# A hybrid decoder layer on one core: operands queued behind sums, the mix of units in the rotation stage, block sums and mixer weights moved

## Chip, cores and metric

One core of one Trainium2 chip runs the whole program in one launch. The metric is the device time in microseconds (us): the median of the runs. A difference of 0.3% is 5.9 us here.

## What is computed

One layer over 1024 tokens of width 1024, all in float32, batch 1:

```python
h = rmsnorm(x, pre_mix_g)
z = h @ w_in      # columns: GLA q|k|v|out gate|forget, conv B|C|x, dilated q|k|v (1536 each)
y_gla = gla_branch(...)                       # chunked gated linear attention, width 512
y_sc = sc_b * causal_dwconv(sc_c * sc_x, sc_conv_w)
y_dil = dilated_branch(rope(d_q), rope(d_k), d_v)   # 3 groups, dilations 1, 4, 16
proj = stack([y_gla, y_sc, y_dil]) @ w_branch       # each branch 512 -> 1024
gates = sigmoid(h @ w_gate + b_gate)                # 3 x 1024 columns
x = x + rmsnorm(sum(gates * proj) @ w_mix_out, post_mix_g)
h = rmsnorm(x, pre_ffn_g)
gt = causal_dwconv(h @ w_ff_gate, ff_conv_w) + ff_conv_b
y = (gelu(gt) * (h @ w_ff_up)) @ w_ff_down          # 1024 -> 2816 -> 1024
x = x + rmsnorm(y, post_ffn_g)
```

The rotation is `x1*cos - x2*sin`, `x2*cos + x1*sin` on the halves of each head of 128 channels.

## The kernel before

**Numbers in two parts.** Every float32 operand of a matmul is held as a high part (`wh`, `H0h`) and a remainder (`wl`, `H0l`) in a reduced format, and a product is three matmuls: high by high, high by remainder, remainder by high. `split` (L158, L159) makes the parts: ScalarE copies the high part, VectorE subtracts it.

**Units of seven products.** Most projections go through `seven` (L275 on): 256 output channels by 1024 tokens are cut in blocks 2x2x2 and done with seven block products of a Strassen kind in place of eight, each of 12 matmuls of 128x512. Sums of the activations' blocks (`TS`) are made once per stage by `block_sums`. Sums of the weights' blocks are made for each unit on GpSimd: s1 (L291), s2 (L293), s1 again (L295, it overwrites s1, so it waits until VectorE has split the old one) and A21 (L297). On TensorE a unit runs: product into X, the last product of the unit before ("rest"), then Y, Z, X, Z, X. Results are collected in SBUF: ScalarE copies X, Z, X (L314, L319, L322), VectorE adds Y (L316), Z (L325) and X (L327). The rest of a unit writes into bank X once more, so TensorE waits there for L327.

**What is done with a result.** `use` takes each of the four 128x512 quarters. Of a light unit (a gate, GLA's q and k) it is an activation and a store. Of a rotation unit (dilated q and k, `rope_out`, L507 to L528) it is: ScalarE swaps the two halves (L517, L518), VectorE multiplies with the cosine (L524), GpSimd multiplies the swapped copy with the sine (L525), VectorE adds the two (L526), and the quarter is stored.

**Stages**, by time in the profiled execution: norm, transposes and the first gates (0 to 88 us), short convolution and gates (88 to 240), tables of cosine and sine (240 to 268), rotations with light units (268 to 670), v of the dilated branch (670 to 795), GLA (795 to 985), dilated attention (985 to 1175), branches merged and mixed, norms (1160 to 1320), first chunk of the feed-forward and its block sums (1310 to 1360), feed-forward units (to 1750), down projection (to the end).

**Order.** Each engine works its instructions in the order in which a scheduler put them when the kernel was built; `issue_after` tells that scheduler to place an instruction behind another one, and is no wait on the chip. GpSimd, VectorE and ScalarE never pass a waiting instruction. In the rotation stage a loop takes a unit from `turned` (12) or `light` (7) by a rule of shares.

**Mixers.** w_mix_out is loaded in quarters of 512x512 by `mix_unit` in the merge stage, and split there: four parts of 128x1024 on GpSimd (L159 with tiles `mw`, two more for `early`), the last on VectorE. `merge` multiplies gates by branch products on VectorE (L1201) and adds them (L1203), on GpSimd for the first four row tiles.

Of the kernel before, what the change touches and what calls it, by code (L numbers as in the profile page):

```python
# [72 lines left out]
def trunk(ctx: ExitStack, tc, x, positions, w_in, w_alpha_up, b_alpha, gla_norm_g, sc_conv_w,  # L73
# [28 lines left out]
    d_fa = dram.tile([FF // 256, 7, 128, 512], F32, name="d_fa")  # L102
    d_st = [dram.tile([48, 128], F32, name=f"d_st{i}") for i in range(4)]
    d_c = [dram.tile([3, T], F32, name=f"d_c{i}") for i in range(4)]

# [139 lines left out]

    def block_sums(B, scratch, Ts):

        f = lambda h, c, j, cs: B[h][c][:, 4 * j:4 * j + 4, cs].bitcast(F32)
        for q in range(2):
            cs = slice(q * 256, q * 256 + 256)  # L250
            f12, t1, f22, t4 = [scratch[:, i].rearrange("p (k t) -> p k t", k=4) for i in range(4)]
            out = lambda i: (Ts[i][:, 0, :, cs], Ts[i][:, 1, :, cs])
            G.tensor_tensor(f12, f(1, 0, 0, cs), f(1, 1, 0, cs), op=OP.add)
            G.tensor_tensor(f22, f(1, 0, 1, cs), f(1, 1, 1, cs), op=OP.add)
            V.tensor_tensor(t1, f12, f(0, 0, 0, cs), op=OP.subtract)
            V.tensor_tensor(t1, t1, f(0, 1, 0, cs), op=OP.subtract)
            split(*out(0), t1)
            G.tensor_tensor(f12, f22, f12, op=OP.subtract)
            V.tensor_tensor(f22, f22, t1, op=OP.subtract)
            split(*out(1), f22)  # L260
            V.tensor_tensor(t4, f(0, 0, 1, cs), f22, op=OP.subtract)
            G.tensor_tensor(t4, t4, f(0, 1, 1, cs), op=OP.add)
            split(*out(2), f12)
            split(*out(3), t4)

    def seven(src, c0, B, Ts, tmp, dst, use):
# [13 lines left out]
        def made(i, src):  # L280
            with ExitStack() as es:
                if sops:

                    for k in ((2, 1) if i < 2 else (3, 4) if i < 4 else (3, 5)):
                        if k in sums_taken:
                            es.enter_context(tc.issue_after(sums_taken[k].ins))
                split(*op(i), src)
# [219 lines left out]
    S.activation(cos, ac, AF.Sin)  # L507
    seven(w_gate2, 8 * 128, H, TS, STMP, ring, gate_out(8))

# [31 lines left out]
    turned = [(w_in2, col + ch, rope_out(w, ch)) for ch in range(0, 1536, 256) for w, col in enumerate((COL_DQ, COL_DK))]  # L541
    light = [(w_gate2, dt * 128, gate_out(dt)) for dt in range(10, 24, 2)]
    nt, n = len(turned), len(turned) + len(light)
    for i in range(n):
        take = turned if (i + 1) * nt // n > i * nt // n else light
        src, c0, use = take.pop(0)
        seven(src, c0, H, TS, STMP, ring, use)
    seven(w_in2, COL_GQ, H, TS, STMP, ring, gla_out(0))
    seven(w_in2, COL_GK, H, TS, STMP, ring, gla_out(1))


    vops = Ring([wp.tile([128, 2, 4, 256], F32R, name=n, tag=n) for n in ("wh", "wl", "wh", "wl")])
    vsrc = [fr[:, i].rearrange("p (k c) -> p k c", k=4) for i in range(4)]
    vsrc = Ring(vsrc + [rawp.tile([128, 4, 256], F32, name="vsrc", tag="raw") for i in range(3)])
    vout = Ring([slot(t, [128, T], name="vout") for t in ("t0", "t1", "t2")])

    def seven_tok(g):
# [51 lines left out]
        store(c11, 0, 0)  # L609
        Z = [pt("g", "vZ") for h in range(2)]  # L610
        prod(Z, op(add(s1, A[1, 0], A[1, 1], OP.add)), tt(0), True)
        c22 = vout()
        copy(c22, Z)
        prod(X, op(add(s1, s1, A[0, 0])), tt(1), False)
        c12 = vout()
        copy(c12, X)
        prod(Z, op(add(A[0, 1], A[0, 1], s1)), blk(1, 1), False)
        plus(c12, Z)
        store(c12, 0, 1)
        prod(X, op(add(A[1, 0], A[0, 0], A[1, 0])), tt(2), False)  # L620
# [584 lines left out]

    v = w_mix2.rearrange("(k p) c -> p k c", p=128)
# [19 lines left out]
    with tc.issue_after(last["d"]):  # L1226
        mix_unit(0, 1, (mw[:, 0], mw[:, 1]), G)
        for d in range(4):
            merge(d, None, (1,))
            ahead(20 + d)  # L1230
        mix_unit(0, 0, early, G)
    for d in range(4, 8):
        ps = gemm((units[8 + d // 2].h, units[8 + d // 2].l), d % 2 * 128, [(k, k) for k in range(4)], X2, "p2")
        queued(merge, d, ps, on=("s", "v"))
        if d == 5:
            mw = slot("G1", [128, 2, 4, 512], F32R, name="mw")
            mix_unit(1, 1, (mw[:, 0], mw[:, 1]), G)
    queued(mix_unit, 1, 0, late, V, on=("s", "v"))

# [167 lines left out]
    def step_operands(i, c):  # L1407
# [144 lines left out]
```

## Time and profile before

| | |
|---|---|
| median of 3 runs | 1967.72 us (1965.96 to 1971.04) |
| profiled execution, own time | 1971.89 us |
| its span | 1970.1 us |
| mean granted TensorE clock | 0.984 |
| TensorE busy | 1891.7 us, 96% of the span |
| VectorE, ScalarE, GpSimd busy | 67%, 44%, 39% |
| moved by DMA | 251.5 MB |

TensorE leaves 78 us of the span idle. The own time is 1.8 us above the span, and 4.2 us above the median of the three timed runs.

### The profile page before, as it was taken

The page shows a single profiled execution, that of the slowest core. Times are in us where ns is not written, and L with a number is a line of the kernel's source. Part 1 is how long each engine was busy: PE and PEld are TensorE (multiplying, and loading weights), DVE is VectorE, ACT ScalarE, POOL GpSimd, SP SyncE. Part 2 cuts the span into 40 slices and gives each one's busy share as a digit, 9 for nine tenths or more (in the row PEclk, how much of TensorE's full clock was granted, in tenths as well). Part 3 has the DMA queues.
Part 4 walks back from the last instruction along what each step waited for, and adds up shares of the span by engine and source line. Part 5 has one row for each costly group of instructions (what it writes and reads, how often), then busy time and mean ns, then how long its engine had stood idle before and what let it go on. Part 6 is the DMA issues. An engine that isn't in the chain of part 4 may idle for free.

```text
span 1970.1 us, 26193 instructions
## 1 busy us (share of the span) xinstructions
PE 1891.7 (96%) x9649; PEld 1601.9 (81%) x9649; DVE 1317.8 (67%) x1927; ACT 876.2 (44%) x1618; POOL 761.4 (39%) x458
## 2 busy tenths in 40 slices
PE   6999999999999999999999898998999999999998
PEld 5988778888777899899788776886788888878887
DVE  7755675677787433567844568577767777778587
ACT  5433355454444332425456623343443444454453
POOL 4523334545454331102214464016445544516162
PEclk9999999999999999999999998999999999999999
DMA  5121323332322433213477554231223232379763
GB/s 175 65 84 66 123 86 109 106 114 100 111 104 91 139 107 120 75 54 102 121 205 227 160 173 152 95 109 59 99 89 121 94 107 91 118 246 322 263 199 123
DMA packets 187074, 251.54 MB, mean 128 GB/s; under 512 B 30018, under 2 KB 121024, under 8 KB 186945
## 3 DMA queue, kind: packets, MB, share of 16 engines
q1 hardware_dynamic: 186944, 249.86, 38.4%
q8 instruction: 76, 1.25, 0.3%
q14 instruction: 54, 0.43, 0.1%
HBM read 183.34 MB, written 66.47 MB: 127 GB/s over the span
## 4 chain that ended last, share of the span: by engine, by line
PE 70%; DVE 14%; issue 5%; POOL 4%; ACT 4%; DMA 3%; SPq 0%; DVEq 0%; ACTq 0%; POOLq 0%
PE sX L307 21%; PE sZ L307 10%; PE sY L307 6%; PE fX L1496 6%; PE fY L1496 4%; PE vX L586 4%; DVE wl L159 3%; PE vZ L586 2%; PE mx L1253 1%; PE mx L1254 1%; PE mx L1252 1%; PE gs L768 1%; PE p L198 1%; POOL fr L525 1%; PE p L200 1%
## 5 line engine op out<-in xcount | busy, mean ns | idle before, releaser
L159 DVE TENSOR_TENSOR wl<-raw,wh 128x512 fp32r<-128x512 f32 (+1 forms) x214 | 215.7, 1044 | 111.4 <-ACT wh L158 108.5
L307 PE MATMUL sX<-T,wh 128*128 128x512 f32 x720 | 227.1, 397 | 10.9 <-DVE ring L327 10.2
L158 ACT ACTIVATE wh<-raw 128x512 fp32r<-128x512 f32 (+1 forms) x226 | 146.2, 671 | 82.2 <-PE sX L307 42.8
L307 PEld LDWEIGHTS sX<-T,wh 128*128 128x128 f32 x720 | 136.7, 191 | 44.0 <-DVE ring L327 14.4
L307 PE MATMUL sX<-FT,wh 128*128 128x512 f32 x480 | 150.1, 394 | 5.9 <-DVE ring L327 4.1
L307 PE MATMUL sX<-T,wl 128*128 128x512 f32 x360 | 142.1, 395 | 0.0
L525 POOL TENSOR_TENSOR fr<-fr 128x512 f32<-128x512 f32 x48 | 70.6, 1471 | 147.7 <-ACT fr L518 146.3
L307 PEld LDWEIGHTS sX<-FT,wh 128*128 128x128 f32 x480 | 89.7, 189 | 28.6 <-DVE ring L327 8.6
L159 DVE TENSOR_TENSOR wl<-fr,wh 128x512 fp32r<-128x512 f32 x90 | 67.0, 766 | 64.3 <-ACT wh L158 63.5
L158 ACT ACTIVATE wh<-fr 128x512 fp32r<-128x512 f32 (+1 forms) x97 | 61.7, 657 | 77.7 <-PE sX L307 49.0
L307 PE MATMUL sX<-FT,wl 128*128 128x512 f32 x240 | 94.1, 392 | 0.0
L291 POOL TENSOR_TENSOR fr<-raw 128x512 f32<-128x512 f32 x30 | 42.0, 1401 | 123.2 <-DMA raw<-in_w_gate_dram 44.6
L159 DVE TENSOR_TENSOR ops<-rw,ops 128x512 fp32r<-128x512 f32 x72 | 62.9, 902 | 30.4 <-ACT ops L158 30.0
L307 PEld LDWEIGHTS sX<-T,wl 128*128 128x128 f32 x360 | 68.8, 191 | 14.8
L297 POOL TENSOR_TENSOR raw<-raw 128x512 f32<-128x512 f32 x50 | 78.3, 1566 | 0.0
L1319 POOL TENSOR_TENSOR fb<-fb 128x512 f32<-128x512 f32 x40 | 61.7, 1543 | 42.4 <-DVE fb L1368 33.9
L526 DVE TENSOR_TENSOR ring<-ring,fr 128x512 f32<-128x512 f32 x48 | 55.2, 1149 | 29.7 <-POOL fr L525 28.2
L307 PE MATMUL sZ<-T,wh 128*128 128x512 f32 x240 | 73.9, 389 | 0.0
L1496 PE MATMUL fX<-ops 128*128 128x512 f32 x312 | 73.2, 389 | 0.0
L1496 PEld LDWEIGHTS fX<-ops 128*128 128x128 f32 x312 | 58.6, 188 | 12.2
L158 ACT ACTIVATE ops<-rw 128x512 fp32r<-128x512 f32 x72 | 43.2, 626 | 55.5 <-PE fX L1496 23.3
L295 POOL TENSOR_TENSOR fr<-raw,fr 128x512 f32<-128x512 f32 x30 | 49.7, 1656 | 46.5 <-DVE wl L159 46.5
(553 smaller groups left out, 5617.4 us busy)
## 6 DMA issues: line engine op xcount, KB each, us to landing
rw<-in_w_ff_down_dram SPq DMA_DIRECT2D x99, 256.0 KB
raw<-in_w_in_dram SPq DMA_DIRECT2D x48, 512.0 KB
rw<-d_fa SPq DMA_DIRECT2D x77, 256.0 KB
d_fa<-fb SPq DMA_DIRECT2D x70, 256.0 KB
raw<-in_w_gate_dram SPq DMA_DIRECT2D x24, 512.0 KB
d_sig<-ring SPq DMA_DIRECT2D x48, 256.0 KB
d_qk<-ring SPq DMA_DIRECT2D x48, 256.0 KB
raw<-in_w_ff_gate_dram SPq DMA_DIRECT2D x22, 512.0 KB
```

Of the source, the lines that this page charges most:

```text
L158: S.activation(h, src, AF.Copy)
L159: eng.tensor_tensor(l, src, h.bitcast(F32), op=OP.subtract)
L198: PE.matmul(ps[h], a, xs[h][0][:, kx, :], start=st, stop=False)
L291: G.tensor_tensor(s1, A21, A22, op=OP.add)
L295: G.tensor_tensor(s1, A12, s2, op=OP.subtract)
L297: G.tensor_tensor(A21, A11, A21, op=OP.subtract)
L307: PE.matmul(ps, a[x][:, k], b[y][:, k], start=first and k == 0 and n == 0, stop=k == 3 and n == 2, skip_group_check=not first)
L525: G.tensor_tensor(sw, sw, sin[:, hs], op=OP.mult)
L526: V.tensor_tensor(as_(o), as_(o), perm(sw), op=OP.add)
L586: PE.matmul(o, b[y][:, k, ts], a[:, x, k], start=first and t % 2 == 0 and k == 0 and n == 0, stop=k == 3 and n == 2, skip_group_check=not ...
L1319: G.tensor_tensor(o, p, q, op=op)
L1496: PE.matmul(P[t], o[:, a, ts], o[:, b], start=st, stop=c + k == NCH - 1 and x == 2, skip_group_check=i not in (2, 1, 5))
```

## The change

1. `made` in `seven` queues each operand's split behind a sum of the unit before in every stage; before, only where `sops` was filled (the feed-forward). Operands 0 and 1 go behind the unit's L319 and L316, 2 and 3 behind L322 and L325, 4 to 6 behind L322 and L327.
2. A second gate unit runs in the stage of the tables, GLA's q and k join the list `light`, and the rule rounds up.
3. The mixers' weights are loaded, split and stored to `d_mw` in 16 steps of 128x512 inside the v stage; `mix_unit` then only loads the finished parts. The steps take the third raw buffer of the v stage.
4. The feed-forward's `block_sums` makes its two f12 sums on VectorE, not on GpSimd.
5. In the down projection operands of all but the first two steps are queued behind the last unit's L327.

```diff
-    def block_sums(B, scratch, Ts):
+    def block_sums(B, scratch, Ts, E=G):
-            G.tensor_tensor(f12, f(1, 0, 0, cs), f(1, 1, 0, cs), op=OP.add)
             G.tensor_tensor(f22, f(1, 0, 1, cs), f(1, 1, 1, cs), op=OP.add)
+            E.tensor_tensor(f12, f(1, 0, 0, cs), f(1, 1, 0, cs), op=OP.add)
...
-            G.tensor_tensor(f12, f22, f12, op=OP.subtract)
+            E.tensor_tensor(f12, f22, f12, op=OP.subtract)
...
         def made(i, src):
             with ExitStack() as es:
-                if sops:
-
-                    for k in ((2, 1) if i < 2 else (3, 4) if i < 4 else (3, 5)):
-                        if k in sums_taken:
-                            es.enter_context(tc.issue_after(sums_taken[k].ins))
+                for k in ((2, 1) if i < 2 else (3, 4) if i < 4 else (3, 5)):
+                    if k in sums_taken:
+                        es.enter_context(tc.issue_after(sums_taken[k].ins))
                 split(*op(i), src)
...
-    seven(w_gate2, 8 * 128, H, TS, STMP, ring, gate_out(8))
+    for dt in (8, 10):
+        seven(w_gate2, dt * 128, H, TS, STMP, ring, gate_out(dt))
...
-    light = [(w_gate2, dt * 128, gate_out(dt)) for dt in range(10, 24, 2)]
+    light = [(w_gate2, dt * 128, gate_out(dt)) for dt in range(12, 24, 2)]
+    light += [(w_in2, COL_GQ, gla_out(0)), (w_in2, COL_GK, gla_out(1))]
...
-        take = turned if (i + 1) * nt // n > i * nt // n else light
+        take = turned if -(-(i + 1) * nt // n) > -(-i * nt // n) else light
...
-    seven(w_in2, COL_GQ, H, TS, STMP, ring, gla_out(0))
-    seven(w_in2, COL_GK, H, TS, STMP, ring, gla_out(1))
...
-    vsrc = Ring(vsrc + [rawp.tile([128, 4, 256], F32, name="vsrc", tag="raw") for i in range(3)])
+    vsrc = Ring(vsrc + [rawp.tile([128, 4, 256], F32, name="vsrc", tag="raw") for i in range(2)])
+    mws = rawp.tile([128, 2, 512], F32R, name="mws", tag="raw")
+
+    def mix_weights():
+
+        v = w_mix2.rearrange("(n i k p) c -> n i k p c", n=1, i=2, p=128)[0]
+        x = mws[:, 0].bitcast(F32)
+        for n in range(2):
+            for i in range(2):
+                for k in range(4):
+                    nc.sync.dma_start(x, v[i, k][:, n * 512:n * 512 + 512])
+                    split(mws[:, 1], mws[:, 0], x)
+                    for part in range(2):
+                        nc.sync.dma_start(d_mw[n, i, part][:, k], mws[:, 1 - part].bitcast(F32))
+                    yield
...
+        next(mixing, None)
...
-    def mix_unit(n, i, pool, eng):
-        mixw[n][i] = wunit([v[:, 4 * i + 2 * j:4 * i + 2 * j + 2, n * 512:n * 512 + 512] for j in range(2)], [4, 512],
-                           pool=pool, eng=eng)
+    def mix_unit(n, i, pool):
+        u = mixw[n][i] = W()
+        u.h, u.l = pool
+        for part in range(2):
+            nc.sync.dma_start(pool[part].bitcast(F32), d_mw[n, i, part])
...
-    queued(mix_unit, 1, 0, late, V, on=("s", "v"))
+    mix_unit(1, 0, late)
...
-    block_sums(F, fb, FT)
+    block_sums(F, fb, FT, V)
...
-        split(o[:, 0], o[:, 1], a)
-        split(o[:, 2], o[:, 3], b)
+
+        with tc.issue_after(sums_taken[5].ins) if len(ready) > 1 else nullcontext():
+            split(o[:, 0], o[:, 1], a)
+            split(o[:, 2], o[:, 3], b)
```

The next two blocks are VectorE's queue over one rotation unit that stands behind a rotation unit (dilation 4 or 16), before and then after the change; the names are tiles, `ring` a quarter, `fr` scratch and tables, `wl<-raw` and `wl<-fr` remainders of the next unit's operands.

```order
L316 TENSOR_TENSOR ring<-ring,sY 128x512
L526 TENSOR_TENSOR ring<-ring,fr 128x512
L524 TENSOR_TENSOR ring<-fr,ring 128x512
L526 TENSOR_TENSOR ring<-ring,fr 128x512
L159 TENSOR_TENSOR wl<-raw,wh 128x512 x2
L159 TENSOR_TENSOR wl<-fr,wh 128x512 x2
L325 TENSOR_TENSOR ring<-ring,sZ 128x512
L524 TENSOR_TENSOR ring<-fr,ring 128x512
L327 TENSOR_TENSOR ring<-ring,sX 128x512
L526 TENSOR_TENSOR ring<-ring,fr 128x512
```

```order
L318 TENSOR_TENSOR ring<-ring,sY 128x512
L529 TENSOR_TENSOR ring<-ring,fr 128x512
L527 TENSOR_TENSOR ring<-fr,ring 128x512
L529 TENSOR_TENSOR ring<-ring,fr 128x512
L161 TENSOR_TENSOR wl<-raw,wh 128x512 x2
L327 TENSOR_TENSOR ring<-ring,sZ 128x512
L161 TENSOR_TENSOR wl<-fr,wh 128x512
L527 TENSOR_TENSOR ring<-fr,ring 128x512
L161 TENSOR_TENSOR wl<-fr,wh 128x512
L529 TENSOR_TENSOR ring<-ring,fr 128x512
L329 TENSOR_TENSOR ring<-ring,sX 128x512
```

The changed file's lines are two or three higher: L161 is the old L159, L318 is L316, L327 is L325, L329 is L327, L527 is L524 and L529 is L526. What moved: the sum of Z stands ahead of both `wl<-fr` splits, and the sum of X now stands behind the rotation's add L529, where it stood ahead of it. In all 12 rotation units X has one such add ahead of it. GpSimd's queue is the same inside a unit: s1, s2, A21, s1 again (L295), then the products with the sine (L525). In sequence the stage was, behind the gate of the tables, L T L T T L T T L T L T T L T T L T T, then q and k (T a rotation, L a light unit); it is now, behind two gates, four times T T L T L, of which the last two L are q and k. Rotations behind a rotation were five, and are four.

Next is GpSimd's queue in the merge stage, before and then after: `mw` and `wl` with L159 are mixer weights, `dE` and `cH1l` belong to the branches, `m_...` and `dB` are merged row tiles.

```order
L1033 TENSOR_TENSOR dD<-dD,cH1l 128x1024
L1036 TENSOR_TENSOR cH1l<-dD 128x1024
L1102 TENSOR_TENSOR dE<-dE,sg 128x1024 x3
L159 TENSOR_TENSOR mw<-raw,mw 128x1024 x2
L1203 TENSOR_TENSOR dB<-dB,m_7233 128x512 x4
L1203 TENSOR_TENSOR m_9064<-m_9064,m_7234 128x512 x2
L1203 TENSOR_TENSOR m_9065<-m_9065,m_7234 128x512 x2
L159 TENSOR_TENSOR wl<-raw,wh 128x1024 x2
L159 TENSOR_TENSOR mw<-raw,mw 128x1024 x2
```

```order
L1061 TENSOR_TENSOR dD<-dD 128x1024
L1058 TENSOR_TENSOR dD<-dD,cH1l 128x1024
L1061 TENSOR_TENSOR cH1l<-dD 128x1024
L1127 TENSOR_TENSOR dE<-dE,sg 128x1024 x3
L1228 TENSOR_TENSOR dB<-dB,m_7314 128x512 x4
L1228 TENSOR_TENSOR m_9145<-m_9145,m_7315 128x512 x2
L1228 TENSOR_TENSOR m_9146<-m_9146,m_7315 128x512 x2
```

The two splits ahead of the merges' adds (L1203, now L1228) and the four behind them are gone; GpSimd's next work are the block sums of the feed-forward.

Last, VectorE's queue where the down projection begins, before and then after: `ops`, `wh<-rw`, `wl<-rw` are its operands, L1368 (now L1394) multiplies a gate.

```order
L316 TENSOR_TENSOR ring<-ring,sY 128x512
L1368 TENSOR_TENSOR fb<-fb,ring 128x512
L159 TENSOR_TENSOR ops<-rw,ops 128x512 x8
L159 TENSOR_TENSOR wh<-rw,wh 128x512
L325 TENSOR_TENSOR ring<-ring,sZ 128x512
L159 TENSOR_TENSOR wh<-rw,wh 128x512
L1368 TENSOR_TENSOR fb<-fb,ring 128x512
L159 TENSOR_TENSOR wl<-rw,wl 128x512 x2
L327 TENSOR_TENSOR ring<-ring,sX 128x512
L1368 TENSOR_TENSOR fb<-fb,ring 128x512
```

```order
L318 TENSOR_TENSOR ring<-ring,sY 128x512
L1394 TENSOR_TENSOR fb<-fb,ring 128x512
L161 TENSOR_TENSOR ops<-rw,ops 128x512 x4
L327 TENSOR_TENSOR ring<-ring,sZ 128x512
L1394 TENSOR_TENSOR fb<-fb,ring 128x512
L329 TENSOR_TENSOR ring<-ring,sX 128x512
L161 TENSOR_TENSOR ops<-rw,ops 128x512
L1394 TENSOR_TENSOR fb<-fb,ring 128x512
L161 TENSOR_TENSOR ops<-rw,ops 128x512 x3
```

Before, twelve operand splits stood ahead of the sum of X (L327, now L329); now four do.

## Rows read from the trace of the kernel before

**Rows 1.** Page, part 1: busy time, share and instructions of each engine.

```profile
PE 1891.7 (96%) x9649; PEld 1601.9 (81%) x9649; DVE 1317.8 (67%) x1927; ACT 876.2 (44%) x1618; POOL 761.4 (39%) x458
```

**Rows 2.** Waits of TensorE: who is waited for: us in total, times, longest us.

```profile
PE sX L307 <- DVE ring L327: 14.3, 9, 2.6
...
PE p L214 <- DVE dB L1201: 8.2, 1, 8.2
```

**Rows 3.** Windows, TensorE, rotation stretch: us, busy (instructions), granted clock, DMA share, GB/s.

```profile
268.00:670.00 402.00, 393.65 (x1697) 0.98 0.33 112
```

**Rows 4.** Timeline, rotation unit behind a light one: start, us, instruction, [idle before <- releaser].

```profile
547.89 1.28 DVE L159 TENSOR_TENSOR wl<-fr,wh 128x512 fp32r<-128x512 f32 x2
...
548.72 1.62 POOL L295 TENSOR_TENSOR fr<-raw,fr 128x512 f32<-128x512 f32 x1 [1.30 <-DVE wl L159]
...
549.10 0.68 DVE L325 TENSOR_TENSOR ring<-ring,sZ 128x512 f32<-128x512 f32 x1
...
551.16 1.29 POOL L525 TENSOR_TENSOR fr<-fr 128x512 f32<-128x512 f32 x1 [0.83 <-ACT fr L518]
...
551.21 0.67 DVE L327 TENSOR_TENSOR ring<-ring,sX 128x512 f32<-128x512 f32 x1
...
551.90 0.39 PE L307 MATMUL sX<-H0h,wl 128*128 128x512 f32 x1
...
552.49 1.07 DVE L526 TENSOR_TENSOR ring<-ring,fr 128x512 f32<-128x512 f32 x1 [0.61 <-POOL fr L525]
```

**Rows 5.** Timeline, TensorE, the unit after it, a rotation behind a rotation.

```profile
573.51 0.73 PE L307 MATMUL sX<-T,wh 128*128 128x512 f32 x2 [2.15 <-DVE ring L327]
```

**Rows 6.** Timeline, a rotation unit of dilation 1: VectorE, TensorE.

```profile
331.96 1.28 DVE L159 TENSOR_TENSOR wl<-fr,wh 128x512 fp32r<-128x512 f32 x2
...
336.12 0.39 PE L307 MATMUL sX<-H0h,wl 128*128 128x512 f32 x1
```

**Rows 7.** Chain that ended last, start, us, two stretches of twelve matmuls.

```profile
573.51 4.62 PE sX L307 x12
...
583.57 2.72 PE sX L307 x12
```

**Rows 8.** Windows, TensorE, behind the wait of rows 5: columns as rows 3.

```profile
574.17:577.58 3.41, 3.41 (x10) 0.51 0.20 77
```

**Rows 9.** Timeline, TensorE, a shorter wait before the tables.

```profile
232.77 0.73 PE L307 MATMUL sX<-T,wh 128*128 128x512 f32 x2 [1.71 <-DVE ring L327]
...
233.57 0.62 PE L307 MATMUL sX<-T,wh 128*128 128x512 f32 x2
```

**Rows 10.** Timeline, merges and mixers' weights: GpSimd, VectorE, TensorE.

```profile
1174.61 4.78 POOL L159 TENSOR_TENSOR mw<-raw,mw 128x1024 fp32r<-128x1024 f32 x2 [6.50 <-ACT mw L158]
...
1185.82 6.84 POOL L1203 TENSOR_TENSOR m<-m,m 128x512 f32<-128x512 f32 x4
...
1193.13 3.37 DVE L159 TENSOR_TENSOR wl<-raw,wl 128x1024 fp32r<-128x1024 f32 x1
...
1200.59 1.30 PE L214 MATMUL p<-dh,wl 128*128 128x512 f32 x2 [8.23 <-DVE dB L1201]
```

**Rows 11.** Timeline, block sums of the feed-forward: GpSimd, VectorE, TensorE.

```profile
1345.46 3.43 POOL L258 TENSOR_TENSOR fb<-fb 128x1024 f32<-128x1024 f32 x1 [1.34 <-DVE fb L255]
...
1322.21 3.40 DVE L255 TENSOR_TENSOR fb<-fb,F0h 128x1024 f32<-128x1024 f32 x1 [2.65 <-POOL fb L253]
...
1344.15 1.23 DVE L255 TENSOR_TENSOR fb<-fb,F0h 128x1024 f32<-128x1024 f32 x1 [2.28 <-POOL fb L253]
...
1355.38 0.50 PE L307 MATMUL sX<-F0h,wh 128*128 128x512 f32 x1 [1.49 <-ACT wh L158]
...
1363.19 0.80 PE L307 MATMUL sY<-F0h,wl 128*128 128x512 f32 x1 [3.27 <-DVE wl L159]
```

**Rows 12.** Timeline, TensorE, start of the down projection.

```profile
1750.50 0.73 PE L307 MATMUL sX<-FT,wh 128*128 128x512 f32 x2 [2.57 <-DVE ring L327]
```

**Rows 13.** Windows, all engines, v stage: busy (instructions) of each, clock, DMA share, GB/s.

```profile
670.00:795.00 125.00, 125.00 (x1025) 124.19 (x1024) 43.95 (x43) 35.45 (x46) 26.72 (x11) 1.00 0.35 113
```

More of the change, by code (lines that the diff above doesn't have):

```diff
@@ L103, in trunk @@
     d_st = [dram.tile([48, 128], F32, name=f"d_st{i}") for i in range(4)]
+    d_mw = dram.tile([2, 2, 2, 128, 4, 512], F32, name="d_mw")
     d_c = [dram.tile([3, T], F32, name=f"d_c{i}") for i in range(4)]
@@ L541, in trunk @@
     turned = [(w_in2, col + ch, rope_out(w, ch)) for ch in range(0, 1536, 256) for w, col in enumerate((COL_DQ, COL_DK))]
-    light = [(w_gate2, dt * 128, gate_out(dt)) for dt in range(10, 24, 2)]
+    light = [(w_gate2, dt * 128, gate_out(dt)) for dt in range(12, 24, 2)]
+    light += [(w_in2, COL_GQ, gla_out(0)), (w_in2, COL_GK, gla_out(1))]
     nt, n = len(turned), len(turned) + len(light)
     for i in range(n):
-        take = turned if (i + 1) * nt // n > i * nt // n else light
+        take = turned if -(-(i + 1) * nt // n) > -(-i * nt // n) else light
         src, c0, use = take.pop(0)
         seven(src, c0, H, TS, STMP, ring, use)
-    seven(w_in2, COL_GQ, H, TS, STMP, ring, gla_out(0))
-    seven(w_in2, COL_GK, H, TS, STMP, ring, gla_out(1))
     vops = Ring([wp.tile([128, 2, 4, 256], F32R, name=n, tag=n) for n in ("wh", "wl", "wh", "wl")])
     vsrc = [fr[:, i].rearrange("p (k c) -> p k c", k=4) for i in range(4)]
-    vsrc = Ring(vsrc + [rawp.tile([128, 4, 256], F32, name="vsrc", tag="raw") for i in range(3)])
+    vsrc = Ring(vsrc + [rawp.tile([128, 4, 256], F32, name="vsrc", tag="raw") for i in range(2)])
[11 more added lines that the diff above has]
+                    yield
+    mixing = mix_weights()
     vout = Ring([slot(t, [128, T], name="vout") for t in ("t0", "t1", "t2")])
@@ L609, in seven_tok @@
         store(c11, 0, 0)
+        next(mixing, None)
         Z = [pt("g", "vZ") for h in range(2)]
@@ L613, in seven_tok @@
         copy(c22, Z)
+        next(mixing, None)
         prod(X, op(add(s1, s1, A[0, 0])), tt(1), False)
@@ L616, in seven_tok @@
         copy(c12, X)
+        next(mixing, None)
         prod(Z, op(add(A[0, 1], A[0, 1], s1)), blk(1, 1), False)
@@ L619, in seven_tok @@
         store(c12, 0, 1)
+        next(mixing, None)
         prod(X, op(add(A[1, 0], A[0, 0], A[1, 0])), tt(2), False)
@@ L622, in seven_tok @@
         store(c22, 1, 1)
+        next(mixing, None)
         o = op(A[1, 1])
@@ L634, in trunk @@
     last_product()
+    assert next(mixing, None) is None
     qk = slot("G0", [128, 4, T], name="gqk")
@@ L1204, in merge @@
                     split(Mg[h][0][:, d], Mg[h][1][:, d], m[:, hs])
-    v = w_mix2.rearrange("(k p) c -> p k c", p=128)
     mixw = [[None, None], [None, None]]
     late, early = [[wp.tile([128, 4, 512], F32R, name=n, tag=n) for n in ("wh", "wl")] for _ in range(2)]
-    def mix_unit(n, i, pool, eng):
-        mixw[n][i] = wunit([v[:, 4 * i + 2 * j:4 * i + 2 * j + 2, n * 512:n * 512 + 512] for j in range(2)], [4, 512],
-                           pool=pool, eng=eng)
+    def mix_unit(n, i, pool):
[3 more added lines that the diff above has]
+            nc.sync.dma_start(pool[part].bitcast(F32), d_mw[n, i, part])
     queued(ahead, 19, on=ALL)
@@ L1226, in trunk @@
     with tc.issue_after(last["d"]):
-        mix_unit(0, 1, (mw[:, 0], mw[:, 1]), G)
+        mix_unit(0, 1, (mw[:, 0], mw[:, 1]))
         for d in range(4):
@@ L1230, in trunk @@
             ahead(20 + d)
-        mix_unit(0, 0, early, G)
+        mix_unit(0, 0, early)
     for d in range(4, 8):
@@ L1236, in trunk @@
             mw = slot("G1", [128, 2, 4, 512], F32R, name="mw")
-            mix_unit(1, 1, (mw[:, 0], mw[:, 1]), G)
-    queued(mix_unit, 1, 0, late, V, on=("s", "v"))
+            mix_unit(1, 1, (mw[:, 0], mw[:, 1]))
+    mix_unit(1, 0, late)
     gb = slot("G2", [128, 4, T], name="gb")
```

## The prediction

> **What bounds the kernel now.** I read the page's busy times first. TensorE is busy 1891.7 of 1970.1 us [rows 1], so a change can only win what is left of its idle time, or lose by adding to it, and every matmul that runs on half the clock counts beside. Then I asked whom TensorE waits for. The largest entry is the sum of X, L327: nine waits, 14.3 us, the longest 2.6; the next that the change touches is one wait of 8.2 us for a merge [rows 2]. In the rotation stage, 402 us long, TensorE is busy 393.65, so 8.35 us are idle there [rows 3]. The timelines of single units show the mechanism: the rest of a unit may start when L327 has ended, and L327 stands in VectorE's queue behind whatever the scheduler put ahead of it.
>
> A wait has a second price. Behind the 2.15 us wait at 573.51 [rows 5] the granted clock is 0.51, the lower level of 1.2 GHz, for some 3.4 us [rows 8]; twelve matmuls then take 4.62 us, in place of 2.72 at full clock [rows 7]. So such a wait costs 1.9 us more. Behind a wait of 1.71 us two matmuls still take 0.62 us [rows 9], which is full speed: no such price there. Between 1.71 and 2.15 these rows leave it open.
>
> **Rotations: the add ahead of X.** This is the term that speaks against the change. The edit is meant to bring sums forward, and it does so for Z, but the order blocks show the add of the rotation, L526, now ahead of L327. That add waits for GpSimd's product with the sine (L525), which stands on GpSimd behind the second s1 (L295), which waits for VectorE's split of the first `wl<-fr`. I lay the old durations in the new order.
>
> A unit behind a light one, dilation 4 or 16 [rows 4]: the raw splits are done at 547.89. Before: X starts at 551.21, ends at 551.88; TensorE's own work ends at 551.90 + 0.39 = 552.29, so there is no wait. After: Z 0.68 (548.57), first `wl<-fr` 0.64, half of 1.28 (549.21), a gap of 0.19 as in the row, L295 1.62 (551.02), L525 1.29 (552.31), gap 0.04, L526 1.07 less the overlap of 0.06 (553.36), X 0.67 (554.03). TensorE resumes 1.75 us late. The cosine product and the second split fit in while GpSimd works. There are five such units: 8.75 us.
>
> Behind a rotation [rows 5] TensorE waits 2.15 us already. X ends 554.03 - 551.88 = 2.15 later by the same insertion, and the queue behind the X of the unit ahead is shorter by the 1.07 of the add that moved in front: 2.15 + 2.15 - 1.07 = 3.2. Three such: 9.7 us. At dilation 1 [rows 6] raw splits are done at 331.96; 0.68 for Z, 0.64, 0.19, 1.62, 1.29, 0.04, an add that I take as long as an X sum [rows 4] (0.67), 0.67 for X: 337.76, against 336.12 + 0.39 = 336.51. That is 1.25, three times: 3.75; for the one of dilation 1 behind a rotation 1.25 plus some of that surplus, 1.7. Sum of the waits 23.9 us. The three of 3.2 halve the clock: 5.7. New cost 29.6. The old one is 8.35 [rows 3] and three waits like that of 2.15 [rows 5] with their 5.7, so 14. **Term: +16 us.** Lower bound: the insertion is half hidden because the raw splits come earlier too, +5. Upper bound: the waits of 1.75 halve the clock as well, six times 1.9, +27. One pair fewer is in these counts. The light units have the same work ahead of X in either order and cost nothing, and the tables keep their surroundings.
>
> **Mixers' weights.** Two splits of 2.4 us go from GpSimd's queue ahead of the merges' adds (4.78 together), and a VectorE split of 3.37 goes too [rows 10]. The adds then start as soon as the products are there, some 2 us earlier (the first of them needs VectorE's products, which ended only during those splits), and the last chain on VectorE loses the 3.37: 5.3 of the 8.23 us that TensorE waits [rows 10]. Less matmul work falls on a halved clock behind a wait that remains, so I add 0.7. **Term: -6 us**, between -2 (the merges are late for their own reasons) and -9 (the whole wait and part of the clock). The added loads, 8 MB in place of 4, have no splits behind them; hidden while the merges last.
>
> In the v stage 16 steps of a load, a split on both engines and two stores are added. VectorE is busy 43.95 of 125 us there, ScalarE 35.45 and the DMA share is 0.35 [rows 13]; the splits are 128x512, so 16 times 0.64 [rows 4], some 10 us, on VectorE, and I take as much on ScalarE. **Term: 0**, upper bound +3. The cover is VectorE's slack; without it each step's splits would cost TensorE directly.
>
> **Feed-forward block sums.** TensorE waits 1.49 and 3.27 us for its first operands [rows 11], which VectorE and ScalarE make only after the block sums; the 3.27 also halve the clock, 1.9: 6.7 together. In the second half GpSimd's difference takes 3.43 us and VectorE waits for it; a sum of that size takes 1.23 on VectorE [rows 11], which is 2.2 less; the first add, behind another one on GpSimd, is off that queue too, and I put another 2 to 3 on it as the same size of work. The operands come 4 to 5 us earlier, which covers the 3.27, its clock and most of the 1.49. **Term: -6 us**, between -2 and -7.
>
> VectorE's sum took 3.40 us where GpSimd had an add in hand, 1.23 where it had none [rows 11]. The Trainium skill, "GPSIMD Engine Reference", section 1 (Specifications), says that GpSimd's SBUF interfaces are shared with VectorE, with contention when VectorE's instruction has two SBUF inputs; the trace agrees, and by that rule f12 on VectorE beside f22 on GpSimd would cost 3.40 and this term would be -4. The same rows carry that without the rule: 2.2 us less gain, inside the bounds.
>
> **Start of the down projection.** L327 stands behind twelve operand splits, now four. The wait of 2.57 [rows 12] goes, and with it a halved clock, at most 1.9 [rows 7]. **Term: -4.3**, between -2 and -4.5. Operands made later are needed seven steps later; what is late next is nothing that I find.
>
> **Sum.** 16 - 6 - 6 - 4.3 = -0.3 against the profiled execution's own 1971.89, which lies 4.2 above the median; against the median 1967.72 it gives 1967.4. I say 1967.
>
> **Rivals.**
> *The add costs little.* The stage goes by +3 or less: the swap on ScalarE starts earlier since Z comes earlier, and if GpSimd's queue let the sine product start before L295, X would be in time. The order speaks against it. It would give 1967.7 + 3 - 16.3 = 1954.
> *Every rotation wait halves the clock* (slower). Place: the rest of each unit behind a light one. Price: 1.9 each for the five of 1.75 and the one of 1.7, 11.4 us, so 1979. It decides from a wait somewhere between 1.71 and 2.15 us; my 1.75 is at the lower edge.
> *The v stage loses its cover.* A split that waits for its load stands ahead of TensorE's operands in VectorE's queue. From some 1 us per step that is not covered, 16 us: 1983.
> *The moved sums do nothing* in the merge and feed-forward stages, because something else ends last there: 1967.4 + 12 less the half that I would still trust, about 1974.
>
> **How the numbers follow.** Forecast 0.42 (1960 to 1975); little cost 0.25 (1949 to 1960); halved clock 0.17 (1974 to 1984); v stage 0.06; sums do nothing 0.10 (1970 to 1979). A difference under 0.3%, 5.9 us, can't be told from none here: the same is 1961.8 to 1973.6. Little cost is faster nearly whole, with a tenth of the forecast's case: faster 0.30. Of the forecast 0.30 and some of the others fall inside: same 0.39. The rest, slower 0.31. The range leaves out a part of the lowest and of the v case: 1952 to 1981.
>
> **What would show it.** Right: twelve waits of 1.2 to 3.3 us for L329 (old L327) in the rotations, each behind an add L529 that waits for GpSimd; idle time there near 24 us in place of 8; no 8 us wait in the merges; the wait for the first X of the feed-forward under 1 us; no wait at the first rest of the down projection. Wrong: rotation waits under 1 us, a halved clock behind waits of 1.7, or waits in the v stage, where TensorE is full now [rows 13].

## The result: slower by 1.3%

The changed kernel took 1992.62 us, median of four runs (1985.98 to 1998.60), against 1968.84 before: a ratio of 1.0126, 95% interval 1.0100 to 1.0152. Forecast were 1967 and a range up to 1981, so the time lies 26 us over the forecast and outside the range. The profiled execution took 1987.92 us. A second set of four runs of the same kernel gave 1987.50 (1975.85 to 1991.42), ratio 1.0098 (1.0062 to 1.0133).

The page of the changed kernel, its span and part 1; busy time answers to [rows 1]:

```profile
span 1986.1 us, 26301 instructions
...
PE 1894.6 (95%) x9649; PEld 1605.6 (81%) x9649; DVE 1321.8 (67%) x1945; ACT 877.9 (44%) x1626; POOL 745.1 (38%) x448
```

TensorE does the same 9649 matmuls; of the 16 us more of span 13 are idle time and 3 are matmuls that took longer. Whom it waits for, the changed kernel (L329 is the sum of X; columns as in [rows 2]):

```profile
PE sX L309 <- DVE ring L329: 34.4, 15, 3.8
...
PE sX L309 <- DVE wl L161: 3.2, 1, 3.2
...
PE p L216 <- DVE dB L1226: 2.7, 1, 2.7
```

The sum of X went from 14.3 to 34.4 us; the merge's wait from 8.2 to 2.7; the 3.2 on a split is at the first feed-forward unit. The rotation stage and the v stage in the changed kernel, by windows (the second row shows all engines):

```profile
268.00:699.20 431.20, 400.35 (x1704) 0.97 0.32 109
...
699.20:831.00 131.80, 131.28 (x1053) 126.55 (x1051) 54.62 (x60) 44.28 (x63) 30.99 (x13) 1.00 0.61 203
```

30.85 us are idle in the rotation stage, where 8.35 were [rows 3]: 22.5 more. The first product of the v stage starts at 699.23, before at 671.81, so the stage grew by 27.4; the other 4.9 are more matmuls on the lower clock. The v stage itself is full of TensorE work, with the mixers' weights in it: 123.7 us to the first product behind it in both profiles. What the later stages give back is read from the first products of the v stage, of the feed-forward's gate and of the down projection, before and then after (that of the down projection after, at 1766.54, is shown with e9 below):

```profile
671.81 0.40 PE L586 MATMUL vX<-wh,H0h 128*128 128x256 f32 x2
...
1308.73 0.48 PE L231 MATMUL fg<-F0h,wh 128*128 128x512 f32 x1
...
1746.19 1.07 PE L1496 MATMUL fY<-ops 128*128 128x512 f32 x4
```

```profile
699.23 0.40 PE L604 MATMUL vX<-wh,H0h 128*128 128x256 f32 x2
...
1329.70 0.48 PE L233 MATMUL fg<-F0h,wh 128*128 128x512 f32 x1
```

The changed kernel is 27.4 us late at the v stage, 21.0 at the feed-forward, 20.4 at the down projection and 16.0 at the end. So between the v stage and the feed-forward, a stretch that ends with the merges and mixers, it wins 6.4 us, in the feed-forward 0.6, and in the down projection 4.3.

One unit behind a light one, dilation 4, on VectorE, GpSimd and TensorE of the changed kernel; it answers to [rows 4]:

```profile
502.52 0.68 DVE L327 TENSOR_TENSOR ring<-ring,sZ 128x512 f32<-128x512 f32 x1
503.12 0.68 DVE L161 TENSOR_TENSOR wl<-fr,wh 128x512 fp32r<-128x512 f32 x1
503.72 1.07 DVE L527 TENSOR_TENSOR ring<-fr,ring 128x512 f32<-128x512 f32 x1
504.71 1.78 DVE L161 TENSOR_TENSOR wl<-fr,wh 128x512 fp32r<-128x512 f32 x1
507.66 1.06 DVE L529 TENSOR_TENSOR ring<-ring,fr 128x512 f32<-128x512 f32 x1 [1.17 <-POOL fr L528]
508.64 0.68 DVE L329 TENSOR_TENSOR ring<-ring,sX 128x512 f32<-128x512 f32 x1
...
503.94 2.00 POOL L297 TENSOR_TENSOR fr<-raw,fr 128x512 f32<-128x512 f32 x1 [1.90 <-DVE wl L161]
505.91 1.72 POOL L528 TENSOR_TENSOR fr<-fr 128x512 f32<-128x512 f32 x1
...
509.38 0.73 PE L309 MATMUL sX<-T,wh 128*128 128x512 f32 x2 [2.19 <-DVE ring L329]
...
532.55 1.22 PE L309 MATMUL sX<-T,wh 128*128 128x512 f32 x2 [3.83 <-DVE ring L329]
```

The last row belongs to the next unit, a rotation behind a rotation. The chain is the one that was laid out: split, second s1, product with the sine, add, sum of X, TensorE. But GpSimd's two links took 2.00 and 1.72 us, where the row of before had 1.62 and 1.29 [rows 4]: VectorE's cosine product and its second split, 1.78 long itself, run beside them. The ends of these four rows show how: cosine product 504.79, second s1 505.94, second split 506.49, product with the sine 507.63. On GpSimd an end comes about 1.15 us behind VectorE's last one, on VectorE 0.55 us behind GpSimd's, although the rows overlap. By these ends the two engines worked in turn, and the overlap is one waiting for the other.

All twelve rotation units wait: 1.55 three times, then 2.25, 3.11, 2.19, 2.19, 3.83, 2.32, 2.33, 3.77 and 2.95, together 29.6 us.

### The profile page after: what moved, and what is told of

It is laid out like the page before. It is cut to its first block, busy times and chain, and to the rows that moved or that the text cites. A ratio compares the mean times of both kernels' runs of the same rounds, so it can differ in the third digit from the quotient of the medians.

```text
span 1986.1 us, 26301 instructions
## 1 busy us (share of the span) xinstructions
PE 1894.6 (95%) x9649; PEld 1605.6 (81%) x9649; DVE 1321.8 (67%) x1945; ACT 877.9 (44%) x1626; POOL 745.1 (38%) x448
## 3 DMA queue, kind: packets, MB, share of 16 engines
q8 instruction: 76, 1.25, 0.3%
## 4 chain that ended last, share of the span: by engine, by line
PE 73%; DVE 11%; POOL 5%; issue 5%; ACT 2%; DMA 2%; SPq 0%; DVEq 0%; POOLq 0%; ACTq 0%
PE sX L309 22%; PE sZ L309 11%; PE sY L309 6%; PE fX L1524 6%; PE fY L1524 5%; PE vX L604 3%; DVE wl L161 3%; PE vZ L604 2%; POOL fr L528 2%; POOL fr L297 1%; PE mx L1280 1%; PE mx L1278 1%; PE mx L1279 1%; PE p L200 1%; PE p L202 1%
## 5 line engine op out<-in xcount | busy, mean ns | idle before, releaser
L161 DVE TENSOR_TENSOR wl<-raw,wh 128x512 fp32r<-128x512 f32 (+1 forms) x212 | 213.4, 1043 | 107.9 <-ACT wh L160 104.0
L160 ACT ACTIVATE wh<-raw 128x512 fp32r<-128x512 f32 (+1 forms) x222 | 142.0, 664 | 88.6 <-PE sX L309 45.6
L161 DVE TENSOR_TENSOR wl<-fr,wh 128x512 fp32r<-128x512 f32 x90 | 71.7, 810 | 71.5 <-ACT wh L160 71.2
L529 DVE TENSOR_TENSOR ring<-ring,fr 128x512 f32<-128x512 f32 x48 | 58.1, 1211 | 54.2 <-POOL fr L528 53.9
L297 POOL TENSOR_TENSOR fr<-raw,fr 128x512 f32<-128x512 f32 x30 | 56.2, 1873 | 65.5 <-DVE wl L161 65.5
L161 DVE TENSOR_TENSOR ops<-rw,ops 128x512 fp32r<-128x512 f32 x72 | 62.3, 894 | 26.7 <-ACT ops L160 26.5
```

What stands on the lines that cost most here:

```text
L160: S.activation(h, src, AF.Copy)
L161: eng.tensor_tensor(l, src, h.bitcast(F32), op=OP.subtract)
L297: G.tensor_tensor(s1, A12, s2, op=OP.subtract)
L529: V.tensor_tensor(as_(o), as_(o), perm(sw), op=OP.add)
```

## The experiments

Three theories stood at the outset: the add ahead of the sum of X makes the loss; the new mix of units makes it; the operands' splits behind the sum of Z make it, through GpSimd. The first four kernels tell them apart.

**e1_no_made.** The queueing of operands is taken back to the feed-forward alone; all else is the changed kernel.

```diff
             with ExitStack() as es:
-                for k in ((2, 1) if i < 2 else (3, 4) if i < 4 else (3, 5)):
-                    if k in sums_taken:
-                        es.enter_context(tc.issue_after(sums_taken[k].ins))
+                if sops:
+                    for k in ((2, 1) if i < 2 else (3, 4) if i < 4 else (3, 5)):
+                        if k in sums_taken:
+                            es.enter_context(tc.issue_after(sums_taken[k].ins))
```

> The changed kernel with the operands' queueing behind sums only in the feed-forward, as before; all else changed. Theory (the rotation's add ahead of the sum of X makes the loss): the rotation stage loses the 27.4 us by which it grew and one wait behind a rotation with its halved clock, about 4, so some 31 below the changed kernel's 1987.9: 1957. Rival (the new mix of units makes the loss): it stays near 1988.

Measured: 1958.40 us, ratio 0.9955 (0.9938 to 0.9971). The waits on the sum of X fell to 9.9 us in seven. As the theory said.

**e2_made_only.** The opposite: the kernel before with the same lines changed the other way and nothing else.

> The kernel before with nothing but the operands queued behind sums in all stages, the old mix of units. Theory: 27 us of rotation waits and their halved clocks, and a fifth pair with about 4 more: 1972 + 31 = 2000 in the profiled execution (1995 to 2005 timed). Rival (the mix of units): near 1970.

Measured: 2002.06 us, ratio 1.0175 (1.0144 to 1.0206). One edit alone costs 35 us; its waits on the sum of X are 37.1 us in sixteen. As the theory said; the mix of units is no part of this loss.

**e3_add_behind_x.** The changed kernel with one placement more.

```diff
-            V.tensor_tensor(as_(o), as_(o), perm(sw), op=OP.add)
+            with tc.issue_after(sums_taken[5].ins) if (i, l) == (0, 1) else nullcontext():
+                V.tensor_tensor(as_(o), as_(o), perm(sw), op=OP.add)
```

> The changed kernel with one more placement: the add of the second quarter's rotation is queued behind the sum of X. Nothing else in VectorE's queue moves, the sum of Z stays early and the operands' splits late. Theory: the rotation waits fall to those of before or under, since the sum of X no longer waits for GpSimd: near 1957. Rival (the splits behind the sum of Z hold GpSimd's second s1 and so everything after it): the waits stay over 1.5 us each, 1980 or more.

Measured: 1959.84 us, ratio 0.9963 (0.9948 to 0.9978). The same place of VectorE's timeline in this kernel:

```profile
484.74 1.78 DVE L161 TENSOR_TENSOR wl<-fr,wh 128x512 fp32r<-128x512 f32 x1
486.44 0.68 DVE L329 TENSOR_TENSOR ring<-ring,sX 128x512 f32<-128x512 f32 x1
487.70 1.09 DVE L530 TENSOR_TENSOR ring<-ring,fr 128x512 f32<-128x512 f32 x1 [0.59 <-POOL fr L528]
```

VectorE still waits for GpSimd, 0.59 us here, but behind the sum of X, and TensorE does not notice. Nothing else in the unit's queue was moved, so it is that add, and not the late splits by themselves.

**e4_sequence_only.** The kernel before with only the new mix of units (the three pieces on `light`, `take` and the second gate in the diff above).

> The kernel before with nothing but the new mix of units: a second gate among the tables, q and k among the rotations, four pairs of rotations in place of five. Theory: one wait of 2.2 us and one halved clock of 1.9 fewer: 1964. Rival (the mix makes the loss): 1985 or more.

Measured: 1967.70 us, ratio 1.0003 (0.9988 to 1.0017). No loss, but also not the 4 us that a pair fewer should bring. TensorE at the entry of the v stage in this kernel, and a window behind it (the number behind the bracket is the granted clock):

```profile
669.68 0.38 PE L586 MATMUL vX<-wh,H0h 128*128 128x256 f32 x1 [1.67 <-ACT wh L158]
672.18 0.58 PE L586 MATMUL vX<-wh,H0h 128*128 128x256 f32 x1 [2.12 <-DVE wh L159]
...
672.20:676.20 4.00, 4.00 (x19) 0.50 0.34 132
```

The last rotation now stands one unit before the v stage, whose first operands are loaded over the cosine and sine tables. Without its wait of 1.67 TensorE would be there at 668.01, against 671.81 before, so the pair fewer did bring nearly 4 us. But the operands come late, 3.8 us in all, and behind the second wait the granted clock is 0.50. The same loads are late in e1 and e3, where they hold ScalarE's copy of the last rotation's X; e1, ScalarE and TensorE:

```profile
668.37 1.06 ACT L160 ACTIVATE wh<-fr 128x1024 fp32r<-128x1024 f32 x1 [5.16 <-DMA fr<-in_w_in_dram]
669.34 0.58 ACT L325 ACTIVATE ring<-sX 128x512 f32<-128x512 f32 x1
...
669.97 0.75 PE L310 MATMUL sX<-T,wh 128*128 128x512 f32 x2 [3.70 <-ACT ring L325]
```

In e3 that wait is 3.51. The changed kernel has no wait there, so the prediction, which gave the mix its gain and the v stage 0, was not tested on this point by its own result.

The next four ask what each other part is worth alone.

**e5_sums_v_only.** The kernel before with the `block_sums` part alone.

> The kernel before with nothing but the feed-forward's f12 sums on VectorE. Theory (VectorE becomes what TensorE waits for: four sums of 1.21 us and its splits of 3.0 and 3.4 beside GpSimd's add stand ahead of the first wl split): the waits at the first feed-forward unit only change place, one wait of about 3.2 us there, within 2 us of before: 1966. Rival (the term of the prediction): 6 less, 1961.

Measured: 1966.29 us, ratio 0.9997 (0.9980 to 1.0014): 0.6 us, with an interval of some 3 us to either side. The wait of 3.2 us is there; the gain is not.

**e8_mix_only.** The kernel before with the mixers' weights in the v stage alone.

> The kernel before with nothing but the mixers' weights split in the v stage (old mix of units, old queueing). Theory (prediction's term): the merges' wait falls from 8.2 to about 2.7 us, the v stage keeps its length, 6 to 7 less: 1960.5. Rival: the steps cost the entry of the v stage what the merges gain: 1967.

Measured: 1960.87 us, ratio 0.9969 (0.9953 to 0.9985): 6.1 us, the theory's number. The merge's wait is 2.72 us, and one of 4.3 stands at the first feed-forward split. This kernel keeps one thing more of the change, GpSimd's two adds in `block_sums` in the new order (f22 ahead of f12), and so do f1_mix_tail and the kernels made from it. The 4.3 stands where the kernel before waits 1.49 and 3.27 [rows 11]; the order of the adds was not tested alone.

**e9_tail_only.** The kernel before with the down projection's queueing alone.

> The kernel before with nothing but the down projection's operands queued behind the last unit's sum of X. Theory: the wait of 2.57 us and its halved clock go, 4.3 less: 1963. Rival: operands made later bring a wait of the same size in the first steps: 1967.

Measured: 1964.09 us, ratio 0.9988 (0.9971 to 1.0004). By the ratio 2.4 us and not clear of nothing; in the profile the wait at the first rest is gone. The traces settle what the times leave open. From the first product of the down projection to the end of the last matmul the kernel before takes 216.8 us; all ten profiles with this edit take 212.5, and the five others without it 215.1 to 216.7. In the changed kernel TensorE at that place, answering to [rows 12], without a bracket, so without a wait:

```profile
1766.54 1.07 PE L1524 MATMUL fY<-ops 128*128 128x512 f32 x4
1767.48 0.72 PE L309 MATMUL sX<-FT,wh 128*128 128x512 f32 x2
```

**f1_mix_tail.** The two parts that held, together, on the kernel before.

> The changed kernel without its rotation parts and without the sums on VectorE: mixers' weights in the v stage and the down projection's queueing, with the old mix of units and the old queueing of operands. Theory: the two terms add, 6 to 7 and 4.3: 1956. Rival: they overlap or the entry of the v stage takes some of it: 1960 to 1962.

Measured: 1958.80 us, ratio 0.9953 (0.9939 to 0.9968): 9.2 us of the expected 11, between theory and rival.

Then the sizes: why the waits are longer than worked out, why times of one kernel spread, and whether a better version is in reach.

**e10_second_split_late.** The changed kernel with the second `wl<-fr` split behind the sum of X.

```diff
-                for k in ((2, 1) if i < 2 else (3, 4) if i < 4 else (3, 5)):
+                for k in ((2, 1) if i < 2 else (3, 4) if i < 3 else (3, 5)):
```

> The changed kernel with the second wl<-fr split queued behind the sum of X, where it no longer runs beside GpSimd's second s1 and product with the sine. Theory (the prediction's durations were those of GpSimd alone, and beside that split they took 2.0 and 1.7 us in place of 1.6 and 1.3): the waits behind light units fall from 2.2 to about 1.6, the pairs from 3.8 to about 3.2, 5 us in all, and some halved clocks go with them: 1980. Rival (the chain is as long without the split, since the cosine product is beside them too): 1988 to 1993.

Measured: 1976.36 us, ratio 1.0050 (1.0037 to 1.0062), 3.6 below what was expected and 11 below the changed kernel's 1987.50 on the same chip. GpSimd in the unit that answers to the one above:

```profile
495.09 2.00 POOL L297 TENSOR_TENSOR fr<-raw,fr 128x512 f32<-128x512 f32 x1 [1.90 <-DVE wl L161]
497.05 1.28 POOL L528 TENSOR_TENSOR fr<-fr 128x512 f32<-128x512 f32 x1
```

The product with the sine is back at 1.28, the duration of before, and the second s1, which still runs beside the cosine product, stays at 2.00. The waits behind light units are 1.71 to 1.84 where they were 2.19 to 2.33, and those of the two later pairs 3.20 to 3.24 in place of 3.77 to 3.83, so the sizing theory holds for that link. The waits on the sum of X fell by 8 us in all. At the entry of the v stage two new waits, of 0.54 and 2.11 us, came up, as in e4.

**after_again.** The changed kernel, unaltered.

> The changed kernel unaltered, for a second profile and more times, because its times fell in two groups (1986 to 1988 and 1997 to 1999) with mean clocks of 0.984 and 0.979. Theory: the waits are equal within 0.1 us from execution to execution, and what differs is behind which waits of 1.5 to 2.4 us the clock halves. Rival: other waits come and go.

Measured: 1987.50 us. The waits of the twelve units agree with the first profile within 0.3 us (one of the three of 1.55 became 1.84, one of 2.19 became 2.47), so the theory's 0.1 was too narrow. Windows of 4 us behind four of the waits, first profile, then second; the number behind the bracket is the granted clock:

```profile
321.50:325.50 4.00, 3.99 (x17) 1.00 0.17 66
...
467.20:471.20 4.00, 4.00 (x11) 0.57 0.17 66
...
532.60:536.60 4.00, 4.00 (x12) 0.64 0.17 66
574.70:578.70 4.00, 4.00 (x18) 1.00 0.17 66
```

```profile
320.30:324.30 4.00, 4.00 (x11) 0.57 0.17 66
...
468.70:472.70 4.00, 4.00 (x18) 1.00 0.17 66
...
532.30:536.30 4.00, 4.00 (x11) 0.61 0.17 66
574.50:578.50 4.00, 4.00 (x18) 1.00 0.17 66
```

Behind a wait of 2.25 us the clock stayed up in the one and fell in the other (2.23); behind 2.19 it fell, behind 2.47 it stayed; behind 3.83 and 3.69 it fell in both; behind 2.32 and 2.31 in neither. Which of the middle waits halve the clock differs from execution to execution, as the theory said, though the waits do too, a little.

**f2_lights_last.** f1_mix_tail with a third mix of units.

```diff
-        take = turned if (i + 1) * nt // n > i * nt // n else light
+        take = turned if "TTLTLTTLTLTTLTLTTLT"[i] == "T" else light
```

> Mixers' weights in the v stage and the down projection's queueing on the kernel before, with a third mix of units: four pairs of rotations, the first pair right behind the tables' gate, and q and k last, so that no rotation stands next but one to the v stage. Theory (the pair fewer is worth 4 us, and the new mix gave it back at the entry of the v stage, where its table must be free): 1955. Rival (the first rotation right behind the tables waits for them): 1959 or more.

Measured: 1956.79 us, ratio 0.9952 (0.9935 to 0.9969). The v stage is entered without a wait; the first rotation has a new one of 2.5 us. Its median is 2 us below that of f1_mix_tail, but the two ran on different chips, and against the kernel before on its own chip each has the same ratio (0.9952 and 0.9953). So no gain over f1_mix_tail is shown.

**f3_difference_v.** f1_mix_tail, with the second of the two f12 sums (the difference) on VectorE and the first on GpSimd.

```diff
-    def block_sums(B, scratch, Ts, E=G):
+    def block_sums(B, scratch, Ts, E=G, D_=G):
...
-            E.tensor_tensor(f12, f22, f12, op=OP.subtract)
+            D_.tensor_tensor(f12, f22, f12, op=OP.subtract)
...
-    block_sums(F, fb, FT)
+    block_sums(F, fb, FT, G, V)
```

> Mixers' weights in the v stage and the down projection's queueing on the kernel before (1958.8), and of the feed-forward's f12 sums the difference alone on VectorE, the add stays on GpSimd. Theory (VectorE's queue is what is full, so half of the moved work costs it half): the wait of 4.3 us at the first feed-forward unit falls to about 3: 1957 to 1958. Rival (GpSimd's chain was the bound): 1954.

Measured: 1953.00 us, ratio 0.9931 (0.9912 to 0.9950), nearer to the rival. But the wait at the first unit stayed, 4.45 us; a later one of 1.82 went. From the first gate product to the down projection the profile is 2.7 us shorter than in f1_mix_tail. The two ran on different chips; by their ratios the step is 4.3 us, but the intervals overlap (0.9912 to 0.9950 and 0.9939 to 0.9968), so its size is open.

**e12_no_taps.** e5_sums_v_only without the shifted taps of the second half's short convolution in the first chunk.

> The kernel before with the feed-forward's f12 sums on VectorE, and the second half of the first chunk's short convolution left out (eight VectorE instructions, some 3.5 us, between the block sums; that part of the output is then the unshifted tap alone). Theory (VectorE's queue is full there, and TensorE's first wl split stands at its end): the wait of 3.2 us at the first feed-forward unit falls under 1 us and its halved clock goes; 5 less than with the convolution: 1961. Rival (the splits wait for GpSimd, ScalarE or a load): the wait stays at 3.

```diff
-            conv(f, ys[f], pg[f], (h,))
+            conv(f, ys[f], pg[f], (h,), h == 0)
```

The new last argument of `conv` says whether the shifted taps are added. Measured: 1963.95 us, ratio 0.9974 (0.9962 to 0.9987), against 0.9997 for e5, so 4.5 us less, though the two intervals touch. Waits of TensorE, e5 and then e12:

```profile
PE sX L307 <- DVE wl L159: 3.2, 1, 3.2
```

```profile
PE sX L307 <- DVE wl L159: 1.0, 1, 1.0
PE sY L307 <- DVE wl L159: 0.9, 1, 0.9
```

3.5 us of unrelated VectorE work less, and the wait falls by 2.2 while a second of 0.9 appears. The stretch from the first gate product to the down projection is 3.2 us shorter. So VectorE's queue is most of what TensorE waits for there; the wait fell to 1.0 us with one of 0.9 behind it, and the times neither show nor rule out the 5 us expected.

**f4_both.** f2_lights_last and f3_difference_v in one kernel.

> Mixers' weights in the v stage, the down projection's queueing, the difference alone of the feed-forward's f12 sums on VectorE, and the mix of units with q and k last: the two versions so far fastest in one kernel. Theory: the terms add, 1951. Rival (no more than one of them shows): 1953 to 1957.

Measured: 1954.72 us, ratio 0.9937 (0.9915 to 0.9959): the rival's number. By the ratios it stands where f3_difference_v does (0.9931), as f2_lights_last stood where f1_mix_tail did; the third mix shows no gain in either place, so whether two gains would add was not tested. f3_difference_v and f4_both are the fastest found, 0.6 to 0.7% under the kernel before, and 1.6 to 2% under the changed kernel's two medians.

## Why the prediction was wrong, step by step

**Rotations, +16: the right mechanism, too small a size.** e2 and e3 show it: that add ahead of that sum costs it. Three things were mis-sized. First, "I lay the old durations in the new order", and with it "The cosine product and the second split fit in while GpSimd works": by the ends of the rows in the result's section they did not fit in, they took turns with GpSimd's work and so stood in the chain. The chain took GpSimd's 1.62 and 1.29 from [rows 4]. The 1.62 was no duration of GpSimd alone either: that s1 began while VectorE's split ran, and ended 1.17 us behind the split's end; one that began beside no VectorE work took 1.28 to 1.30 (e10). In the new order the two took 2.00 and 1.72, 0.8 us more in a unit, of which the raw splits, ending earlier, gave back some: 1.75 was forecast behind a light unit and 2.19 to 2.33 measured; 3.2 behind a rotation, and 3.11, 3.83 and 3.77 measured; at dilation 1, 1.25 and 1.7, and 1.55 and 2.25. The sum of waits is 29.6, not 23.9. e10 shows the share of the split beside the sine product. Second, the last rotation before the v stage, counted as 1.75, waits 2.95; a mixers' split stands ahead of its raw splits on VectorE, and ScalarE waits 1.28 us for that split's load, but no experiment took that apart. In kind it is the rival "The v stage loses its cover", at one place and ahead of the v stage. Third, the clock: with 2.2 us the waits lie in the stretch that [rows 5, 9] left open, and behind some of them it is halved: behind five of the twelve waits in the first profile, six in the second, the windows show a clock under 0.7. The term was 27.4 in the profile, just over its upper bound of 27. The median run is 4.7 us slower than the profiled one; in which stage is not known. On the other side the old cost of 14 was about 1 us too high, since the 8.35 of [rows 3] hold the end of a wait for Z at 268.97 that the changed kernel has too.

**The rival "every rotation wait halves the clock"** (17 in 100) named the right place and sign and gave 1979. It came partly true, for five and six of the twelve waits, on top of longer waits. It rested on a length of wait between 1.71 and 2.15 us at which the clock falls; the runs show no such length (last section), and the trace of before had the lower clock behind a wait of 1.98 at 512.28 already. No case of the prediction joined two failures. The rotations' upper bound and a feed-forward term of 0 together give 1967.4 + 11 + 6 = 1984, over the range's 1981, and both came.

**Mixers' weights, -6: right.** 6.1 alone (e8), and 6.4 between the v stage and the feed-forward in the changed kernel. The merge's wait fell by 5.5, where 5.3 was worked out, and the v stage took the steps without a wait.

**Feed-forward block sums, -6: wrong.** About 1 or nothing: 0.6 by the ratio of e5, and 0.6 in the stage in the changed kernel's profile. The step that failed is "The operands come 4 to 5 us earlier". It followed GpSimd's chain and left out that VectorE gains four sums of 1.2 us and that its splits grow to 3.0 and 3.4 beside GpSimd's add. VectorE, GpSimd and TensorE of the changed kernel ahead of the late split (`wl<-raw`):

```profile
1355.52 3.03 DVE L161 TENSOR_TENSOR FT<-fb,FT 128x1024 fp32r<-128x1024 f32 x1
...
1359.60 3.41 DVE L161 TENSOR_TENSOR FT<-fb,FT 128x1024 fp32r<-128x1024 f32 x1
...
1374.27 1.22 DVE L264 TENSOR_TENSOR fb<-F0h,fb 128x1024 f32<-128x1024 f32 x1
1375.40 0.68 DVE L1371 TENSOR_TENSOR fy<-fy,fg 128x512 f32<-128x512 f32 x1
1376.00 4.14 DVE L161 TENSOR_TENSOR wl<-raw,wh 128x512 fp32r<-128x512 f32 x2
...
1355.07 2.39 POOL L265 TENSOR_TENSOR fb<-fb,F0l 128x1024 f32<-128x1024 f32 x1 [11.08 <-DVE fb L264]
1358.62 3.31 POOL L256 TENSOR_TENSOR fb<-F1h,F1l 128x1024 f32<-128x1024 f32 x1 [1.16 <-DVE FT L161]
1375.56 2.34 POOL L265 TENSOR_TENSOR fb<-fb,F0l 128x1024 f32<-128x1024 f32 x1 [13.63 <-DVE fb L264]
...
1378.51 0.76 PE L309 MATMUL sX<-F0h,wl 128*128 128x512 f32 x1 [3.23 <-DVE wl L161]
```

No row of VectorE here has an idle bracket: the queue is full, and the operand that TensorE waits for stands at its end. The two engines take turns here as well. The 3.03 ends 1.09 us behind GpSimd's add of 1355.07, the 3.41 1.08 behind that of 1358.62, and so do 15 of the 16 sums and splits of 128x1024 on VectorE that began within an operation of GpSimd in this trace (1.1 us behind its end; alone they take 1.2); at the 16th GpSimd's ended 1.15 us behind VectorE's. So 1.9 us of the late split, from 1376.00 to GpSimd's end at 1377.90, are waiting for GpSimd's last add. The Trainium skill, "GPSIMD Engine Reference", section 1 (Specifications), says that GpSimd's SBUF interfaces are shared with VectorE, with contention when a VectorE instruction has two SBUF inputs; the split at 4.14 for two, beside GpSimd's add, agrees, where a lone one took 0.68 (at 503.12 above). The prediction priced that rule at 2 us of this term and did not carry it to the rotations, where it was worth 0.8 us a unit.

**Start of the down projection, -4.3: right in the profiles**, where the wait is gone and the stage 4.3 us shorter each time; the times of e9 show 2.4 with an interval that reaches zero.

**What was not foreseen** is the entry of the v stage: the new mix alone gains one pair and loses 3.8 us there (e4). The changed kernel hid it behind the rotation waits: where these are shorter, in e1, e3 and e10, the late loads show.

## What to carry to other kernels

When a scheduler's edit moves one instruction forward, read which waiting instruction is now ahead of the one that the bounding engine needs: here an early sum of Z let the scheduler put an add that waits for another engine ahead of the sum of X. Durations taken from an old order hold only with the same neighbours: at the places shown VectorE's sums and splits and GpSimd's work took turns, so lay such work end to end, and look whether a long row in the old order holds waiting. Work moved from an idle engine to one that is fuller, on a path where the fuller engine's last instruction is awaited, gives back what it saves.

## What the runs showed of the hardware that was not expected

Waits of TensorE between 1.8 and 2.5 us are followed by the lower clock in one execution and not in another, at the same place of the same program: 1.84 did (402 us of the second profile), 2.47 did not. In the rotations of these two profiles 1.55 us never did, 2.9 and more always did; but in e10 a wait of 3.24 us did not, and the window behind it shows full clock:

```profile
522.70:526.70 4.00, 4.00 (x18) 1.00 0.17 66
```

So in these runs the length of one wait does not decide. Within the eight runs of the changed kernel, 1975.85 to 1998.60 us, the mean clock is 0.988 in the fastest, 0.979 in the two slowest and 0.981 to 0.985 in between. The kernel before, with fewer such waits, spread over 8 to 14 us in series of 13 to 30 runs, a series of the changed kernel over 13 and 16 in four runs each.

VectorE's sums and splits and GpSimd's operations, where their rows overlap at the places shown, ended one behind the other, the later one by a little less than it takes alone: 0.55 us of 0.68 and 1.09 of 1.22 on VectorE, 1.15 of 1.28 on GpSimd. A sine product on GpSimd, 128x512, took 1.28 us with VectorE waiting and 1.72 beside VectorE's split, of which 1.14 lay behind the split's end.
